# A hybrid encoder on one core: order of the down products, norm and gate loads at the layer boundary, scratch in two pools

## The chip, the cores and the metric

The kernel runs on one core of a Trainium2 chip. The metric is the device time of one execution in microseconds (us). A core has five engines that work side by side: PE (TensorE, matmuls; PEld is its loading of weights), DVE (VectorE), ACT (ScalarE), POOL (GpSimd) and SP (SyncE, which here only issues DMAs). Each runs its own list of instructions in order and waits on semaphores for the others.

## The reference

Two layers on x, 256 tokens of 2048 features, in fp32:

```
x = x + attention(rmsnorm(x));  x = x + swiglu(rmsnorm(x))     # layer 0
x = x + recurrent(rmsnorm(x));  x = x + swiglu(rmsnorm(x))     # layer 1
rmsnorm(x) = x * rsqrt(mean(x*x) + 1e-6) * g
swiglu(h)  = (silu(h @ w_gate) * (h @ w_up)) @ w_down          # 2048 -> 5632 -> 2048
recurrent(h): xb, gb = split(h @ w_in); xb = conv of width 4 (xb)
              a, i = gates of xb (blocks of 256 features, sigmoid)
              scans forward and backward, summed, times gelu(gb), then @ w_out
```

## The kernel before

**Precision and tiles.** Each fp32 operand is split into a high part (fp32r, a cast) and a low part (the rest); a product is three matmuls, high x high, high x low, low x high. Features lie in tiles of 128: 16 tiles for 2048. The 5632 hidden features of the FFN come in three parts of 12, 16 and 16 tiles (`PARTS`). A part is made of units of four tiles, each unit a pair of columns of 512 (one of w_gate, one of w_up), and is then multiplied by its rows of w_down, whose four columns of 512 are added to x (`x_tok`, tokens in partitions).

**Weights.** They stream in halves of 512 KB: SP issues the load (L114, tile raw, five buffers), ACT casts the high part (L123, hi), DVE subtracts the low part (L124, lo). PE uses a half for 12 matmuls of 128x512.

**project_pair** (matmul L294) multiplies a pair of columns at once: steps over k, one half per column and step, into two banks of sums (acc) per column. At the steps of `SEVEN` (2 and 5) it uses one level of Strassen: seven products instead of eight, from sums of the weights (wx on DVE, wxh a cast on ACT L271, wxl on DVE L272) and sums of the operands (hf); `merge` (L333 on) adds the results up into fg and fu. `pair_plan` gives the order: both columns in turn up to the last step of `SEVEN`, then one column's remaining two steps after the other's. **project_tokens** (matmul L247) multiplies one column by itself, one half after the other. `down` uses pairs for the 16-tile parts; the 12-tile part goes through `output`, which calls project_tokens column by column.

**Units.** At its end a unit turns its result by blocks (`turned`: DVE transposes into tb, L462, then 16 copies into tf, L468 on DVE and L470 on ACT) and splits it into four tiles (act; L795 on ACT, L796 on DVE), which the down product reads.

**Norm.** The norm before the recurrent layer (`nr`) works column by column while the last down ends: `add` squares (L426) and turns column c of x and writes four operands (xg; L418 on ACT, L419 on DVE). After the last column, `finish` takes the root (Ln and Exp on ACT, L541, three small operations on DVE, L484 to L486); `spread` scales the identity by it (ndg, L444) and puts a matmul with ones (L450) into PE's order after `NORM` tile steps; its result nrb (copied at L452) scales the projections afterwards.

**Recurrent layer.** Block 0's two feature tiles are projected first (`project_two`, matmuls L341 to L343, three of 128x256 per tile step): k tiles 0 to 7 for both, 8 to 11 for both, then 12 to 15, which are the operands of the last norm column. `conv_branch` does the convolution (L827 to L832) and splits the result (xs, L378 and L379). `load_gates` loads a gate's weights on SP (graw, L855), casts them on ACT (ghi, L856) and subtracts on POOL (glo, L857); four are loaded ahead. Gate products (three matmuls per tile, into pm) enter PE's order after `WHEN` tile steps of the projections that follow.

**Order and memory.** PE's order is the order of the program; `later(n, fn)` puts work into it n tile steps further on. The other engines are put in order by a scheduler that models the program. `follow` gives it an order without a semaphore. The FFN's scratch is one pool (`fp`: tb, tf, wx, fg, fu, forms), closed at the end of layer 0's FFN; the recurrent layer's pool (`rp`) is opened in the same place, so its first buffers wait for what lay there. The functions that the diff touches follow.

Of the kernel before, what the change touches and what calls it, by code (L numbers as in the profile page):

```python
# [18 lines left out]
P = 128  # L19
# [12 lines left out]
LAST_STEPS = (0, 1, 3, 2, 4, 5, 6, 7)  # L32
# [4 lines left out]
COMMON = {"nsq", "nr", "nrt", "rsq_s", "nj", "ndg", "nrb"}  # L37
EPS = 1e-6
# [5 lines left out]
NORM = 26  # L44
# [7 lines left out]
WHEN = (18, 25, 32, 39, 42, 46, 50, 54, 58, 60, 62, 64, 66, 70, 74)  # L52
WHEN_LAST = (5, 9, 13, 17, 19, 20, 21, 24, 24, 25, 26, 27, 33, 39, 39)
# [20 lines left out]
def trunk(ctx, tc, w, out):  # L74
# [60 lines left out]
    def pair_plan(steps, apart):  # L135
        m = 1 + steps.index(SEVEN[-1]) if apart else len(steps)
        return [(n, (0, 1)) for n in steps[:m]] + [(n, (j,)) for j in range(2) for n in steps[m:]]

    def unit_steps(first):
        return FIRST_STEPS if first else USUAL_STEPS, True  # L140

    def down_steps(p, second):
        last = p == len(PARTS) - 1
        return LAST_STEPS if second and last else USUAL_STEPS, True

    def ffn_order(l):
        units = [wide(f"w_gate{l}"), wide(f"w_up{l}")]
        seq, i = [], 0
        for p, n in enumerate(PARTS):
            for _ in range(n // FOUR):  # L150
                for k, cols in pair_plan(*unit_steps(i == 0)):
# [3 lines left out]
            if n != KT:  # L155
                seq += down
                continue
            for c in range(0, len(down), n):
                for k, cols in pair_plan(*down_steps(p, c > 0)):
                    seq += [down[c + n // 2 * j + k] for j in cols]  # L160
        return seq
# [95 lines left out]
    def seven_forms():  # L257
        load_half(*order[taken[0]])
        r1, w1 = flat(newest["raw"]), [flat(t) for t in newest["tiles"]]
        x, xh, xl = (fp[0].tile([P, 3, WIDE], t, tag=n, name=nm(n), bufs=1) for n, t in (("wx", F32), ("wxh", F32R), ("wxl", F32R)))  # L260

        def sums(raw):
            r2 = flat(raw)
            dve.tensor_tensor(x[:, 0, :], r2[:, 0, :], r1[:, 0, :], ALU.add)  # L264
            dve.tensor_tensor(r2[:, 0, :], r2[:, 0, :], r2[:, 1, :], ALU.add)
            dve.tensor_tensor(x[:, 1, :], r2[:, 0, :], r1[:, 0, :], ALU.add)
            dve.tensor_tensor(x[:, 2, :], x[:, 1, :], r1[:, 1, :], ALU.add)  # L267

# [3 lines left out]
        dve.tensor_tensor(xl, x, xh[:].bitcast(F32), ALU.subtract)  # L272
        taken[0] += 2
        return [[t[:, k, :] for t in w] for w, k in ((w1, 0), (w1, 1), (w2, 0), (w2, 1), ((xh, xl), 0), ((xh, xl), 1), ((xh, xl), 2))]

    def x_forms(h0, h1, tag):
        y = fp[0].tile([P, 8, P], F32, tag="tb", name=nm("tb"))
        for i, h in enumerate((h0, h1)):
            o, hi, lo = y[:, 2 * i : 2 * i + 2, :].rearrange("p a t -> p (a t)"), h[:, :S].bitcast(F32), h[:, S:].bitcast(F32)
            dve.tensor_tensor(o, hi, lo, ALU.add)  # L280
        for o, a, b in ((4, 1, 3), (5, 0, 4), (6, 0, 1), (7, 2, 5)):
            dve.tensor_tensor(y[:, o, :], y[:, a, :], y[:, b, :], ALU.subtract)
        t = fp[0].tile([P, 2, 4, P], F32R, tag=tag, name=nm(tag), bufs=1)
# [4 lines left out]
    def project_pair(xs, forms, order, middle, done):  # L288
        banks = [[new_acc() for _ in range(2)] for _ in range(2)]
        begun = set()  # L290

# [10 lines left out]
        steps = pair_plan(*order)  # L302
        seven = [n for n in order[0] if n in forms]
        for n, cols in steps:
            if n in forms:
# [6 lines left out]
                product(banks[0][0], tokens(2 * n + 1, 0), b21)  # L312
                product(banks[1][0], s4, b22)
# [3 lines left out]
                product(banks[0][1], tokens(2 * n + 1, 1), t4)  # L317
                if last:
                    middle(p1, q5, q6, q7)
            else:  # L320
                for j in cols:
                    half()
                    hi, lo = (flat(t) for t in newest["tiles"])
                    end = n == order[0][-1]
                    for a in range(2):
                        for k in range(2):
                            product(banks[j][a], tokens(2 * n + k, a), (hi[:, k, :], lo[:, k, :]), end and k == 1)
                    if end:
                        done(j, banks[j])

    def merge(p1, q5, q6, q7):
        g, u = (fp[0].tile([P, 2, WIDE], F32, tag=t, name=nm(t), bufs=1) for t in ("fg", "fu"))
# [72 lines left out]
    class Norm:  # L405
# [28 lines left out]
        def finish(self):  # L434
# [3 lines left out]
            self.rt = rsqrt(ms, "nr")  # L438


        def spread(self):
            dg = tmp("ndg", bufs=1)
            for a in range(2):
                dve.tensor_scalar(dg[:, a * P : (a + 1) * P], ident, self.rt[:, a : a + 1], None, ALU.mult)  # L444
# [8 lines left out]

            later(NORM, stage)

    def turned(src, both=True):
# [4 lines left out]
        for q in range(4):  # L463
            for i in range(4):
                o, y = f[32 * i : 32 * i + 32, q::4, :, :], b[32 * q : 32 * q + 32, :, i, :]
                y = y.rearrange("p a (k t) -> p a k t", k=FOUR)
                if i % 2 and both:
                    dve.tensor_copy(o, y)  # L468
                else:
                    act.copy(o, y)  # L470
# [4 lines left out]
    def open_ffn():  # L475
        fp[:] = [ffn_scope.enter_context(tc.tile_pool(name=nm("fp"), bufs=1))]
# [13 lines left out]
    def output(xs, norm=None, end=False, ready=0, close=None):  # L490
# [12 lines left out]
        if norm is not None:  # L503
            norm.finish()


    def down(xs, forms, p, norm=None, end=False):
        for c in (0, 2):
# [19 lines left out]
            project_pair(xs, forms, down_steps(p, c > 0), middle, done)  # L528
        if norm is not None:
            norm.finish()  # L530
# [244 lines left out]
    def ffn(norm, nxt):  # L775
        def unit(hid, forms, first):
# [12 lines left out]
            project_pair(norm.xs, norm.forms, unit_steps(first), lambda *banks: got.extend(merge(*banks)), done)  # L789
# [8 lines left out]
            for i, n in enumerate(SEVEN):  # L798
                if forms is not None and first <= 2 * n < len(hid):
                    forms[n] = x_forms(hid[2 * n], hid[2 * n + 1], f"hf{i}")  # L800

        for p, n in enumerate(PARTS):
            hid, forms = [], {} if n == KT else None
            for i in range(n // FOUR):
                unit(hid, forms, p == i == 0)
# [3 lines left out]
            if n == KT:  # L809
                down(hid, forms, p, nxt if last else None, last and nxt is None)  # L810
            else:
                output(hid)
# [4 lines left out]
    nr.spread()  # L817
# [3 lines left out]
    scope.append(rt.enter_context(tc.tile_pool(name="rp", bufs=2)))  # L821
# [99 lines left out]
    for b in range(-1, NBLK):  # L921
        blk, nxt = nxt, Block(b + 1) if b + 1 < NBLK else None
        if blk:
# [4 lines left out]
            when = WHEN if nxt else WHEN_LAST  # L928
# [11 lines left out]
    def end_recurrence():  # L940
        rt.close()
        scope.pop()
# [91 lines left out]
```

## Time and profile before

| | |
|---|---|
| median of 3 runs | 2022.96 us (2022.78 to 2024.07) |
| the profiled execution's own time | 2022.37 us |
| its span in the trace | 2020.6 us |
| PE busy | 1995.2 us (99%), 9944 matmuls |
| DVE, ACT, POOL busy | 1666.0, 1320.7, 165.7 us |
| mean granted PE clock | 0.993 |
| moved by DMA | 386.06 MB, 191 GB/s on the mean |

Times inside the trace count from the start of the span; the execution's own time is 1.8 us more than the span. In rows of groups and of the timeline, `out<-in` are the program's names, `x8` is a count, and what stands in brackets is the idle time before and the engine and line that ended it. In rows of waits stand the total, the number and the longest. The granted clock is PE's, as a share of full speed. Matmuls overlap, so the distance of their starts, and not their durations, is what one costs.

### The profile page before, as it was taken

What the parts mean: (1) busy time and instruction counts of PE and PEld (TensorE: products, weight loads), DVE (VectorE), ACT (ScalarE), POOL (GpSimd) and SP (SyncE); (2) the same over time, 40 slices, a digit from 0 to 9 for tenths busy, and PEclk for the clock granted to TensorE, in tenths of its full rate; (3) what the DMA queues carried; (4) which work ended last, traced back from release to release, by engine and by line L of the source; (5) the groups of instructions that cost most, each with busy time, mean ns of one, the idle gap of its engine ahead of it and who ended that gap; (6) DMA issues with size and microseconds to landing.
All of it is one profiled execution on the core that took longest, in us unless ns stands there. A gap on an engine that the chain in (4) does not pass through costs nothing.

```text
span 2020.6 us, 27860 instructions
## 1 busy us (share of the span) xinstructions
PE 1995.2 (99%) x9944; PEld 1696.2 (84%) x9944; DVE 1666.0 (82%) x2347; ACT 1320.7 (65%) x2054; POOL 165.7 (8%) x213
## 2 busy tenths in 40 slices
PE   9999999999999999999899999999999999999999
PEld 8898888878888888887799998888788888888887
DVE  8998788856888888889868887898657898878897
ACT  7666666644667546677688898667545766457663
POOL 1463000000000000000133330000000000000000
PEclk9999999999999999999999999999999999999999
DMA  8444665656555665555555555655566566665564
GB/s 320 158 137 140 193 200 187 207 168 198 192 195 187 219 208 188 190 195 192 188 163 188 178 179 174 200 188 187 195 185 202 185 204 206 203 192 187 196 222 146
DMA packets 109004, 386.06 MB, mean 191 GB/s; under 512 B 12225, under 2 KB 12993, under 8 KB 108737
## 3 DMA queue, kind: packets, MB, share of 16 engines
q1 hardware_dynamic: 108720, 384.26, 58.0%
q8 instruction: 78, 1.28, 0.3%
q14 instruction: 62, 0.50, 0.1%
q10 hardware_dynamic: 144, 0.02, 0.0%
HBM read 382.13 MB, written 2.10 MB: 190 GB/s over the span
## 4 chain that ended last, share of the span: by engine, by line
PE 52%; issue 41%; DVE 4%; DMA 1%; ACT 1%; POOL 0%; DVEq 0%; SPq 0%; ACTq 0%; POOLq 0%
PE acc L294 24%; PE acc L247 7%; PE acc L225 6%; PE pm L294 4%; PE acc L341 3%; PE acc L342 3%; PE acc L343 3%; DVE lo L124 2%; PE pm L342 1%; PE pm L343 1%; PE pm L341 1%; DMA raw<-in_w_up_dram 1%; ACT hi L123 0%; DMA graw<-in_w_gates_dram 0%; ACT tf L470 0%
## 5 line engine op out<-in xcount | busy, mean ns | idle before, releaser
L123 ACT CAST hi<-raw 128x1024 fp32r<-128x1024 f32 (+1 forms) x708 | 730.4, 1045 | 486.1 <-PE acc L294 314.1
L124 DVE TENSOR_TENSOR lo<-raw,hi 128x1024 fp32r<-128x1024 f32 (+1 forms) x708 | 857.4, 1228 | 172.0 <-ACT hi L123 169.9
L294 PE MATMUL acc<-hi,xg 128*128 128x512 f32 x2200 | 694.4, 389 | 2.3 <-DVE fg L783 1.2
L294 PEld LDWEIGHTS acc<-hi,xg 128*128 128x128 f32 x2200 | 412.9, 188 | 91.0 <-DVE fg L783 2.0
L294 PE MATMUL acc<-lo,xg 128*128 128x512 f32 x1100 | 427.9, 389 | 0.0
L247 PE MATMUL acc<-hi,act 128*128 128x512 f32 x896 | 283.4, 395 | 6.2 <-ACT act L795 5.4
L294 PE MATMUL acc<-hi,act 128*128 128x512 f32 x800 | 252.7, 389 | 0.0
L294 PEld LDWEIGHTS acc<-lo,xg 128*128 128x128 f32 x1100 | 206.5, 188 | 42.4
L247 PEld LDWEIGHTS acc<-hi,act 128*128 128x128 f32 x896 | 170.7, 191 | 43.8 <-ACT act L795 6.3
L470 ACT COPY tf<-tb 32x256 f32<-32x256 f32 x448 | 180.8, 403 | 12.7 <-DVE tb L462 6.1
L294 PEld LDWEIGHTS acc<-hi,act 128*128 128x128 f32 x800 | 150.2, 188 | 32.3 <-issue 0.7
L247 PE MATMUL acc<-lo,act 128*128 128x512 f32 x448 | 176.8, 395 | 0.0
L294 PE MATMUL acc<-lo,act 128*128 128x512 f32 x400 | 155.6, 389 | 0.0
L342 PE MATMUL acc<-xg,hi 128*128 128x256 f32 x512 | 146.7, 286 | 2.0 <-DVE xg L419 1.9
L341 PE MATMUL acc<-xg,hi 128*128 128x256 f32 x512 | 146.8, 287 | 1.0 <-ACT xg L418 1.0
L343 PE MATMUL acc<-xg,lo 128*128 128x256 f32 x512 | 146.2, 285 | 0.0
L264 DVE TENSOR_TENSOR wx<-raw,raw 128x512 f32<-128x512 f32 x60 | 41.5, 692 | 123.7 <-DMA raw<-in_w_up_dram 97.1
L225 PE MATMUL acc<-xg,hi 128*128 128x512 f32 x384 | 127.1, 400 | 0.5 <-ACT hi L123 0.5
L271 ACT CAST wxh<-wx 128x1536 fp32r<-128x1536 f32 x60 | 88.9, 1482 | 49.6 <-DVE wx L267 46.7
L272 DVE TENSOR_TENSOR wxl<-wx,wxh 128x1536 fp32r<-128x1536 f32 x60 | 104.8, 1747 | 10.5 <-ACT wxh L271 10.5
L342 PEld LDWEIGHTS acc<-xg,hi 128*128 128x128 f32 x512 | 99.7, 195 | 2.5 <-DVE xg L419 2.4
L341 PEld LDWEIGHTS acc<-xg,hi 128*128 128x128 f32 x512 | 99.8, 195 | 1.5 <-ACT xg L418 1.3
(239 smaller groups left out, 2728.4 us busy)
## 6 DMA issues: line engine op xcount, KB each, us to landing
raw<-in_w_gate_dram SPq DMA_DIRECT2D x176, 512.0 KB, 4.0
raw<-in_w_up_dram SPq DMA_DIRECT2D x176, 512.0 KB, 4.4
raw<-in_w_down_dram SPq DMA_DIRECT2D x176, 512.0 KB, 4.2
raw<-in_w_in_dram SPq DMA_DIRECT2D x64, 512.0 KB, 4.6
raw<-in_w_qv_dram SPq DMA_DIRECT2D x40, 512.0 KB, 4.3
raw<-in_w_o_dram SPq DMA_DIRECT2D x32, 512.0 KB, 3.6
raw<-in_w_out_dram SPq DMA_DIRECT2D x32, 512.0 KB, 4.3
graw<-in_w_gates_dram SPq DMA_DIRECT2D x32, 256.0 KB, 3.6
```

Source lines behind the costliest of these rows:

```text
L123: newest["cast"] = act.copy(hi[:, sl, :], raw[:, sl, :])
L124: dve.tensor_tensor(lo[:, sl, :], raw[:, sl, :], hi[:, sl, :].bitcast(F32), ALU.subtract)
L225: pe.matmul(o, w, x, start=(k == 0 and not part), stop=(k == total - 1 and not part))
L247: pe.matmul(accs[a], x, wt[:, k, :], start=(k0 + k == 0 and n == 0), stop=(end and k == 1 and n == 2))
L264: dve.tensor_tensor(x[:, 0, :], r2[:, 0, :], r1[:, 0, :], ALU.add)
L271: act.copy(xh, x)
L272: dve.tensor_tensor(xl, x, xh[:].bitcast(F32), ALU.subtract)
L294: pe.matmul(acc, a, b, start=id(acc) not in begun, stop=last and i == 2)
L341: pe.matmul(o, hi, x[:, :S], start=start, stop=False)
L342: pe.matmul(o, hi, x[:, S:], start=False, stop=False)
L343: pe.matmul(o, lo, x[:, :S], start=False, stop=stop)
L470: act.copy(o, y)
```

## The change

1. The 12-tile down of either layer goes through `down`, so in pairs, without seven forms: four steps for both columns, then the last two column by column (`SHORT`, `down_plan`). Banks of sums are taken when first used.
2. Layer 0's last down takes its second pair of columns without seven forms and one column after the other (`alone`). `LAST_STEPS`, an order of steps for the last downs' second pairs, is gone.
3. The root (`finish`) is taken in `add` of the last column, ahead of its block copies; for `nr` the diagonal (`spread`) too, and the copies on ACT follow the Exp, those on DVE the diagonal. `NORM` is 20 instead of 26.
4. The FFN's scratch is two pools, `fq` (tb, tf) and `fp` (the rest), and the recurrent layer's too, `rq` (cb, xc, gl) and `rp` (the rest).
5. Block 0's four gates enter PE's order after 24, 30, 36 and 42 tile steps instead of 18, 25, 32 and 39.

```diff
-LAST_STEPS = (0, 1, 3, 2, 4, 5, 6, 7)
+SHORT = 6
+LOW = {"cb", "xc", "gl"}
-NORM = 26
+NORM = 20
+WHEN_FIRST = (24, 30, 36, 42) + WHEN[4:]
...
-        pl = tp if tag in COMMON else scope[-1]
+        pl = tp if tag in COMMON else scope[-2] if tag in LOW else scope[-1]
...
+    def pair_plan(steps, together):
+        return [(n, (0, 1)) for n in steps[:together]] + [(n, (j,)) for j in range(2) for n in steps[together:]]
...
+    def down_plan(n, alone):
+        if alone:
+            return pair_plan(range(n), 0)
+        return pair_plan(range(n), SHORT - 2 if n == SHORT else 1 + SEVEN[-1])
...
-        x, xh, xl = (fp[0].tile([P, 3, WIDE], t, tag=n, name=nm(n), bufs=1) for n, t in (("wx", F32), ("wxh", F32R), ("wxl", F32R)))
+        x, xh, xl = (fp[1].tile([P, 3, WIDE], t, tag=n, name=nm(n), bufs=1) for n, t in (("wx", F32), ("wxh", F32R), ("wxl", F32R)))
...
-        banks = [[new_acc() for _ in range(2)] for _ in range(2)]
+        banks = [[], []]
+        def bank(j, a):
+            while len(banks[j]) <= a:
+                banks[j].append(new_acc())
+            return banks[j][a]
...
         def add(self, c):
             for a in range(2):
                 act.activation(tmp("nj", (P, WIDE), bufs=1), x_tok[:, a, c, :], AF.Square, accum_out=self.sums[:, a, c : c + 1])
-            for f in turned(x_tok[:, :, c, :]):
+            behind = self.finish() if c == NCOL - 1 else None
+            for f in turned(x_tok[:, :, c, :], True, behind):
...
             self.rt = rsqrt(ms, "nr")
+            if not self.seven:
+                return prev[0], self.spread()
...
+                turn = dve.tensor_copy if i % 2 and both else act.copy
+                n = turn(o, y)
+                if behind is not None:
+                    follow(n, behind[i % 2])
...
-        fp[:] = [ffn_scope.enter_context(tc.tile_pool(name=nm("fp"), bufs=1))]
+        fp[:] = [ffn_scope.enter_context(tc.tile_pool(name=nm(s), bufs=1)) for s in ("fq", "fp")]
...
-            project_pair(xs, forms, down_steps(p, c > 0), middle, done)
-        if norm is not None:
-            norm.finish()
+            alone = norm is not None and c > 0
+            project_pair(xs, {} if alone else forms, down_plan(len(xs) // 2, alone), middle, done)
...
-            if n == KT:
-                down(hid, forms, p, nxt if last else None, last and nxt is None)
-            else:
-                output(hid)
+            down(hid, forms, nxt if last else None, last and nxt is None)
...
     ffn_scope.close()
-    nr.spread()
...
-    scope.append(rt.enter_context(tc.tile_pool(name="rp", bufs=2)))
+    scope.extend([rt.enter_context(tc.tile_pool(name=s, bufs=2)) for s in ("rq", "rp")])
...
-            when = WHEN if nxt else WHEN_LAST
+            when = WHEN_FIRST if not blk.b else WHEN if nxt else WHEN_LAST
```

Three places show what this moves. The first is PE in layer 0's 12-tile down; the numbers tell buffers apart; hi and lo are the parts of a half of w_down, act_3986 (after: act_3989) is the last tile of the second unit, act_4332 (after: act_4335) the first of the third. Before:

```order
L247 MATMUL acc_4345<-hi_4401,act_3986 128x512
L247 MATMUL acc_4345<-lo_4402,act_3986 128x512
L247 MATMUL acc_4345<-hi_4401,act_3986 128x512
L247 MATMUL acc_4344<-hi_4419,act_4332 128x512
L247 MATMUL acc_4344<-lo_4420,act_4332 128x512
```

and after:

```order
L299 MATMUL acc_4380<-hi_4478,act_3989 128x512
L299 MATMUL acc_4380<-lo_4479,act_3989 128x512
L299 MATMUL acc_4380<-hi_4478,act_3989 128x512
L299 MATMUL acc_4353<-hi_4496,act_4335 128x512
L299 MATMUL acc_4353<-lo_4497,act_4335 128x512
```

Before, the third unit's first tile is read after four halves of one column, 48 matmuls into the down; after, it is read after four halves of either column, 96 matmuls into it.

The second is ACT where layer 0's last down ends; nj are the squares, tf the block copies of column 3, xg its operands, the rows that write rsq_s and nr the Ln and the Exp. Before:

```order
L426 ACTIVATE nj_9075,nsq_3278<-x_tok 128x512
L123 CAST hi_9392<-raw_9391 128x1024
L470 COPY tf_9078<-tb_9077 32x2x128 x8
L418 ACTIVATE xg_9097<-tf_9078,pk 128x256
L418 ACTIVATE xg_9100<-tf_9078,pk 128x256
L418 ACTIVATE xg_9103<-tf_9078,pk 128x256
L418 ACTIVATE xg_9106<-tf_9078,pk 128x256
L541 ACTIVATE rsq_s_9113<-nrt_9109 128x2
L541 ACTIVATE nr_9112<-rsq_s_9113 128x2
L856 CAST ghi_9294<-graw_9295 128x512
L452 COPY nrb_9249<-pm_9246 128x256
```

and after:

```order
L430 ACTIVATE nj_9051,nsq_3281<-x_tok 128x512
L125 CAST hi_9329<-raw_9328 128x1024
L546 ACTIVATE rsq_s_9057<-nrt_9053 128x2
L546 ACTIVATE nr_9056<-rsq_s_9057 128x2
L476 COPY tf_9067<-tb_9066 32x2x128 x8
L125 CAST hi_9372<-raw_9371 128x1024
L459 COPY nrb_9211<-pm_9208 128x256
L422 ACTIVATE xg_9086<-tf_9067,pk 128x256
L422 ACTIVATE xg_9089<-tf_9067,pk 128x256
L422 ACTIVATE xg_9092<-tf_9067,pk 128x256
L422 ACTIVATE xg_9095<-tf_9067,pk 128x256
```

Ln and Exp have moved ahead of the copies, the norm's copy nrb ahead of the operands, and no gate cast stands here.

The third is SP's queue of loads: raw are halves of weights, graw the gates' weights. Before:

```order
L114 DMA raw_9634<-in_w_in_dram 128x1024
L114 DMA raw_9672<-in_w_in_dram 128x1024
L855 DMA graw_9295<-in_w_gates_dram 128x512
L855 DMA graw_9301<-in_w_gates_dram 128x512
L855 DMA graw_9307<-in_w_gates_dram 128x512
L855 DMA graw_9313<-in_w_gates_dram 128x512
L114 DMA raw_9722<-in_w_in_dram 128x1024
L855 DMA graw_9418<-in_w_gates_dram 128x512
```

and after:

```order
L116 DMA raw_8809<-in_w_down_2_dram 128x1024
L856 DMA graw_9275<-in_w_gates_dram 128x512
L856 DMA graw_9281<-in_w_gates_dram 128x512
L116 DMA raw_8827<-in_w_down_2_dram 128x1024
L116 DMA raw_8845<-in_w_down_2_dram 128x1024
L856 DMA graw_9287<-in_w_gates_dram 128x512
L116 DMA raw_8901<-in_w_down_2_dram 128x1024
L856 DMA graw_9293<-in_w_gates_dram 128x512
L116 DMA raw_8921<-in_w_down_2_dram 128x1024
L856 DMA graw_9416<-in_w_gates_dram 128x512
```

Before, the gate loads stand behind the first twelve loads of w_in; after, six of them stand among the second half of the loads of layer 0's last w_down; the sixth follows one load behind the last row.

More of the change, by code (lines that the diff above doesn't have):

```diff
@@ L300, in tokens @@
             return [xs[k][:, o + a * P : o + (a + 1) * P] for o in (0, S)]
-        steps = pair_plan(*order)
-        seven = [n for n in order[0] if n in forms]
-        for n, cols in steps:
+        seven = [n for n, cols in plan if n in forms]
+        for n, cols in plan:
             if n in forms:
@@ L775, in ffn, with unit @@
     def ffn(norm, nxt):
-        def unit(hid, forms, first):
+        def unit(hid, forms, parts, first):
             got = []
@@ L941, in end_recurrence @@
         rt.close()
-        scope.pop()
+        del scope[-2:]
         ln_exp_tables()
```

71 lines of the change are left out of this document (29 added, 42 removed).

## The prediction

> **What bounds the kernel now.** I read the busy times first, then what TensorE (PE) waited for, then busy times by stretch, and last single places in order of time.
>
> ```profile
> span 2020.6 us, 27860 instructions
> PE 1995.2 (99%) x9944; PEld 1696.2 (84%) x9944; DVE 1666.0 (82%) x2347; ACT 1320.7 (65%) x2054; POOL 165.7 (8%) x213
> ...
> 418.00:950.00 532.00, 531.71 (x2344) 439.45 (x2343) 441.25 (x538) 329.16 (x447) 0.00 (x0) 1.00 0.60 196
> 1014.50:1200.00 185.50, 185.50 (x1556) 185.50 (x1555) 152.45 (x249) 165.23 (x281) 69.39 (x87) 1.00 0.57 179
> ```
>
> PE is the bound, and over long stretches it has no gap. A stretch's row gives its length, then busy time and instructions of PE, PEld, DVE, ACT and POOL, then the granted clock. The first stretch holds 128x512 matmuls: one takes 532.00 / 2344 = 0.227 us. The second holds 128x256 ones: 185.50 / 1556 = 0.119 us. So the time falls only with fewer matmuls or with less lost between them. Where is it lost?
>
> ```profile
> PE acc L247 <- ACT act L795: 5.4, 2, 2.7
> PE pm L294 <- DVE wxl L272: 2.2, 1, 2.2
> PE acc L342 <- DVE xg L419: 1.9, 1, 1.9
> PE pm L341 <- DVE xs L378: 1.8, 1, 1.8
> PE pm L341 <- ACT hi L123: 1.7, 1, 1.7
> PE acc L294 <- DVE fg L783: 1.2, 2, 0.6
> PE acc L294 <- DVE fu L786: 1.2, 4, 0.4
> PE pm L450 <- DVE ndg L444: 1.1, 1, 1.1
> ...
> 406.00:418.00 12.00, 8.76 (x25) 6.18 (x24) 6.27 (x9) 6.15 (x11) 0.00 (x0) 0.72 0.38 133
> 950.00:956.00 6.00, 3.81 (x18) 2.81 (x17) 5.96 (x9) 1.84 (x2) 0.00 (x0) 1.00 0.70 238
> 982.00:997.00 15.00, 10.88 (x59) 9.86 (x58) 10.61 (x28) 9.80 (x25) 0.50 (x5) 0.77 0.44 142
> 1003.60:1014.50 10.90, 7.03 (x34) 6.16 (x34) 9.67 (x16) 5.77 (x9) 3.11 (x6) 0.69 0.62 198
> 1447.00:1459.00 12.00, 9.04 (x26) 6.38 (x25) 5.88 (x8) 6.52 (x12) 0.00 (x0) 0.72 0.40 132
> ```
>
> A wait's row gives total, times and longest. The large ones lie in the five stretches below them, and in four of these the clock sinks to about 0.7: such a wait costs more than itself. By the pitches, 406 to 418 needs 25 x 0.227 = 5.7 us of its 12.0: 6.3 are lost; 1447 to 1459 needs 5.9, so 6.1. There the down product of the first FFN part (12 tiles) starts, in either layer. 982 to 997 needs 55 x 0.119, and about 0.06 for each of four short matmuls of the norm, together 6.8: 8.2 lost. 1003.6 to 1014.5 needs 34 x 0.119 = 4.05: 6.85 lost. These two are the start of the recurrent layer and its first gates.
>
> **Part A: the 12-tile down in pairs.**
>
> ```profile
> 400.33 6.63 ACT L470 COPY tf<-tb 32x256 f32<-32x256 f32 x16 [0.72 <-DVE tb L462]
> 406.99 1.99 ACT L123 CAST hi<-raw 128x1024 fp32r<-128x1024 f32 x2
> 408.89 1.32 ACT L795 CAST act<-tf 128x256 fp32r<-128x256 f32 x4
> ...
> 410.34 1.43 DVE L796 TENSOR_TENSOR act<-tf,act 128x256 fp32r<-128x256 f32 x4
> ...
> 406.25 0.39 PE L247 MATMUL acc<-hi,act 128*128 128x512 f32 x1
> 409.34 0.51 PE L247 MATMUL acc<-hi,act 128*128 128x512 f32 x1 [2.71 <-ACT act L795]
> ```
>
> From 406.25 PE stands before tile 8, which the last unit hands over only after 16 block copies and two casts of halves; its last low part ends at 410.34 + 1.43 = 411.8. Before the change 48 matmuls of the down stand ahead of tile 8, after it 96. So the down starts at about 406.5 - 48 x 0.227 = 395.6, and tile 8 is needed at 395.6 + 96 x 0.227 = 417.4, 5.6 us after its last part is there. What hides the wait is 48 more matmuls on tiles that are ready; a half of the weights still serves 12 matmuls (2.72 us), so the loads keep their pace, and ACT and DVE keep their order up to these casts. I count the loss as gone: -6.3 and -6.1, **-12.4**. Bounds: nothing saved if PE waits elsewhere; 0.4 more at each place, since matmuls cut by a stretch's edges are counted whole.
>
> What it adds: a pair holds four banks of sums where a column held two. The rows of L783 and L786 are such waits at the starts of pairs: 2.4 us in all over some 30 pairs, 0.08 a pair. With six more starts (four pairs in the 12-tile downs, two single columns at the end of layer 0) I take **+0.4**; bounds 0 and 6 x 0.6 = 3.6.
>
> **Part B: layer 0's last pair without seven forms, a column at a time.**
>
> ```profile
> 952.21 1.75 DVE L272 TENSOR_TENSOR wxl<-wx,wxh 128x1536 fp32r<-128x1536 f32 x1
> ...
> 951.43 0.39 PE L294 MATMUL pm<-wxh,hf 128*128 128x512 f32 x1
> 954.01 0.50 PE L294 MATMUL pm<-wxl,hf 128*128 128x512 f32 x1 [2.19 <-DVE wxl L272]
> ```
>
> One matmul goes from 951.43 to 954.01: 2.58 - 0.23 = 2.35 lost. No sums, no wait: -2.35. Each form spares one product in eight, three matmuls, so two forms less add 6 x 0.227 = +1.36. Together **-1.0**. What is late next is a low part of a half, which DVE writes beside the norm of column 1; with DVE rid of 1.75 us of wxl and four additions for each form I put that at nothing, and bound it by the old wait, +2.35.
>
> **Part C: the boundary.** T is the end of the last down.
>
> ```profile
> 986.34 3.30 ACT L470 COPY tf<-tb 32x256 f32<-32x256 f32 x8 [0.77 <-DVE xg L419]
> 990.02 1.71 ACT L418 ACTIVATE xg<-tf,pk 128x256 fp32r<-128x256 f32 x4 [0.38 <-DVE tf L468]
> 991.63 0.19 ACT L541 ACTIVATE rsq_s<-nrt 128x2 f32<-128x2 f32 x1
> ...
> 980.58 0.69 DVE L522 TENSOR_TENSOR x_tok<-x_tok,acc 128x512 f32<-128x512 f32 x1
> 987.54 2.38 DVE L468 COPY tf<-tb 32x256 f32<-32x256 f32 x8
> ...
> 977.04 0.28 PE L341 MATMUL acc<-xg,hi 128*128 128x256 f32 x1
> ```
>
> Before, T is 977.04. Columns 2 and 3 end only two halves (5.4 us) apart, so column 2's copies and operands still hold both engines after T: column 3 is added to x only at 980.58 + 0.69 (T+4.2), its ACT copies start at T+9.3, its operands at T+13, and the root behind them at T+14.6. After, column 2 ends eight halves (8 x 2.72 = 21.8 us) ahead of T and is out of the way. My chain from T: both additions by T+1.0, squares, casts and transposes to T+3.8, Ln and Exp (two of 0.2) to T+4.5, ACT's eight copies (3.3) to T+7.8, a cast (1.05) and the norm's copy (0.4) to T+9.2, four operands (1.7) to T+10.9; on DVE root, diagonal and copies (2.4) to T+8.8, a low half (1.2), the four low parts (1.7) to T+11.7. PE multiplies operands 0 to 11 first, 72 matmuls of 0.119 and the norm's four: it asks for operand 12 at T+9 and for its low part at once, each of the four coming some 0.4 us late. I take 1.5 us of waits for 8.2: **-6.7**. Bounds: 0 left, or half of 8.2.
>
> The norm's matmuls, moved 6 tiles earlier, come at T+7.2 and want the diagonal of T+6.4: no wait in place of the 1.1 us.
>
> ```profile
> 992.64 6.96 SPq L855 DMA_DIRECT2D graw<-in_w_gates_dram  x4
> ...
> 996.70 2.55 POOL L857 TENSOR_TENSOR glo<-graw,ghi 128x512 fp32r<-128x512 f32 x2 [4.05 <-ACT ghi L856]
> 1003.78 1.54 POOL L857 TENSOR_TENSOR glo<-graw,ghi 128x512 fp32r<-128x512 f32 x1 [0.59 <-ACT ghi L856]
> ...
> 1004.12 1.36 DVE L378 CAST xs<-xc 128x256 fp32r<-128x256 f32 x1
> 1008.24 0.29 DVE L378 CAST xs<-xc 128x256 fp32r<-128x256 f32 x1
> ```
>
> At the first gates PE waited for a half (1.7) and for xs (1.8). The four gate loads were issued from 992.64 only, since their buffers lay on tb and tf; so four casts (0.62 each) and four subtractions on POOL stood among the convolution's work, and beside POOL one cast on DVE took 1.36 for 0.29. After, the loads go out during the last down, and that work is done before T. The gates come six tiles (6 x 3 x 0.119 = 2.1 us) later as well. The chain from T puts the second xs at T+23.3 and the first gate at T+22.1 to 22.5: about 0.8 us left of 6.85, **-6.0**. Bounds: 0, or the waits' 3.5 - 2.1 = 1.4 with the slow clock, some 3.
>
> The four POOL subtractions now stand beside DVE's last column. The row of 1.36 shows 1.07 us lost at one of them. The Trainium skill, "SBUF — State Buffer", section "Who interferes with whom", says that a GpSimd operation that reads SBUF shuts out a DVE operation with two SBUF inputs for its whole length. The row agrees with a block to the end of the subtraction (1003.78 + 1.54 = 1005.3). It speaks against the change, since DVE has the low halves to write there.
>
> **The sum.** -12.4 + 0.4 - 1.0 - 6.7 - 6.0 = -25.7 on the profiled execution's own 2022.37: 1996.7. The median shown, 2022.96, is 0.6 above it: **1997.2**. Restoring the natural order of steps in layer 1's last pair costs nothing: the same order runs without loss in the pairs of 418 to 950.
>
> **The rivals.**
> 1. *The boundary keeps half* (0.22): the copies now follow the root, so operand 12 is late by the whole of the root's delay, and the clock sinks again. For it: a wait of 1.9 came before a stretch of 0.77. Against: the 2.19 at 951 left the clock at 1.00, and mine come in pieces. Half of 8.2 + 6.85 is 7.5, where I count 2.3: +5.2, 2002.4. The Trainium skill, "TensorE: Matmul & The Clock Gate", Part 1, has half rate only after an idle window of about 3.4 us; by it these waits would cost only themselves. The rows speak against it: 2.71 was enough at 409.
> 2. *POOL shuts out DVE* (0.08) in the last column, four times 1.3 = 5.2 us; ACT's column 2 work with its casts is some 23.7 us by these rows, which leaves a low half some 2.4 us of the ring's cover, so PE waits 2.8: 2000.0.
> 3. *The pairs only move the wait* (0.07), as 4 tiles of the last unit still come late or the banks are held: +12.4, 2009.6. Against: 5.6 us to spare.
> 4. *The gate loads stop the stream* (0.05): on SP's queue the six now stand among the last down's halves, and each waits for a buffer that POOL or DVE frees.
>
> ```profile
> SPq L855 <- POOL glo L857: 33.0, 28, 3.5
> ```
>
>    Such a wait is 1.2 on the mean, 3.5 at most. Five raw buffers hold 5 x 2.72 = 13.6 us of PE's work. To end slower than before, the six must hold the queue 13.6 + 25.7 = 39.3 us, 6.6 each; at 7.5 each the loss is 45 - 13.6 = 31.4, and the time 2028.6. Against: twice the longest seen.
> 5. *It does nothing here* (0.01): 2023. The order of the matmuls excludes it nearly.
>
> **How the numbers follow.** My forecast has 0.57, 1993 to 2000.5: the bounds of what is left (0 to 2.3 at the boundary) and of the banks. Rivals 1 and 2 lie up to 2005, with the slow clock once more; so 1993 to 2005 holds about 0.85, and I leave out rivals 3, 4 and 5. A measurement tells 0.2%, 4 us, from no change. Faster by more: 0.57 + 0.22 + 0.08 + 0.07 = 0.94, less 0.01 for rivals worse than priced: 0.93; within: 0.02; slower: 0.05.
>
> **What would show it.** A: no wait of PE for act and clock 1.00 through 395 to 420 and at the second layer's down; wrong if a wait for act, hi or lo of over 1 us stands there. B: no wxl behind column 1; six matmuls more. C: root ahead of copies, waits for xg below 2 us together, clock 1.00 behind T; gate loads and subtractions before T, casts on DVE at 0.29, and the wait at the first gate under 1 us. Wrong as a whole if SP's queue shows waits of the gate loads above 5 us with PE waiting for hi or lo in the last down.

## The result, and the profile after

The changed kernel takes 1995.07 us (median of 4 runs, 1994.69 to 1996.29); the kernel before takes 2022.87 us (median of 4 runs, 2021.08 to 2024.07). The ratio is 0.9864, 95% interval 0.9847 to 0.9881: 27.8 us, 1.4% faster. The forecast was 1997.2 in a range of 1993 to 2005.

The lines of the page and the waits of TensorE (PE) in the changed kernel. Its source lines stand some five further down: L299 is the matmul of pairs (before L294), L345 to L347 those of the recurrent layer (L341 to L343), L788 and L791 the bank readers of a unit (L783 and L786), L528 those of a down.

```profile
span 1993.1 us, 27849 instructions
PE 1981.8 (99%) x9950; PEld 1686.4 (85%) x9950; DVE 1652.8 (83%) x2329; ACT 1317.0 (66%) x2051; POOL 168.6 (8%) x213
...
PE acc L299 <- DVE fg L788: 1.0, 2, 0.5
PE pm L401 <- POOL ones L398: 1.0, 1, 1.0
PE acc L225 <- ACT hi L125: 0.9, 1, 0.9
PE acc L299 <- DVE x_tok L528: 0.9, 1, 0.9
PE acc L299 <- DVE fu L791: 0.7, 3, 0.3
PE pm L346 <- DVE pT L725: 0.7, 1, 0.7
PE acc L346 <- DVE xg L423: 0.6, 1, 0.6
```

The waits for act, wxl, xs, hi at the gates and ndg have gone from the list; the six matmuls more are there (9950 for 9944). What is left at the places of the change is one wait for xg. New is one of 0.9 us for x_tok, a bank not yet read; it stands at 1695.82, in a 16-tile down of layer 1. The same five stretches, found by their work (start of the 12-tile downs, end of layer 0's last down, boundary, first gates):

```profile
395.00:420.00 25.00, 25.00 (x112) 20.71 (x111) 15.53 (x19) 17.03 (x30) 0.00 (x0) 1.00 0.57 187
900.00:968.90 68.90, 68.90 (x306) 57.05 (x305) 63.25 (x92) 51.55 (x86) 6.97 (x4) 1.00 0.68 225
968.90:985.00 16.10, 15.35 (x124) 14.87 (x123) 14.22 (x32) 12.86 (x26) 0.20 (x4) 1.00 0.44 152
985.00:996.00 11.00, 11.00 (x93) 10.84 (x92) 10.18 (x19) 6.57 (x9) 1.63 (x7) 1.00 0.65 207
1417.00:1445.00 28.00, 28.00 (x125) 23.20 (x124) 17.31 (x21) 17.92 (x30) 0.00 (x0) 1.00 0.60 200
```

PE is without a gap in four of the five, and the granted clock is 1.00 in all of them.

To see where the 27.5 us of the two profiled executions (2022.37 and 1994.88) went, I took six marks from PE's starts: the first matmul of layer 0's FFN; T, the first 128x256 matmul behind its last down; the 96th and the 250th 128x256 matmul from T on (the boundary, then the first gates); the first matmul of layer 1's FFN and the last matmul.

| from mark to mark, us | before | after | difference |
|---|---|---|---|
| layer 0's FFN, to T | 708.88 | 701.68 | -7.20 |
| T to the 96th | 20.14 | 13.22 | -6.92 |
| the 96th to the 250th | 25.50 | 18.60 | -6.90 |
| the 250th to layer 1's FFN | 286.86 | 286.62 | -0.24 |
| layer 1's FFN, to the last matmul | 706.87 | 701.06 | -5.81 |

Up to layer 0's FFN the difference is -0.6; nothing is changed there. These marks serve for the experiments too. A stretch in which the program is the same varies by up to 3 us from execution to execution (layer 1's FFN took 701.06 in the changed kernel, 699.91 in e3 and 702.81 in e5, which do not touch it), and the waits for fu and x_tok vary with it. So an edit of 1 us is read at its own place, not in the median.

The chain behind T in the changed kernel, in order of time (start, duration, engine):

```profile
973.15 0.20 ACT L546 ACTIVATE rsq_s<-nrt 128x2 f32<-128x2 f32 x1
973.38 0.20 ACT L546 ACTIVATE nr<-rsq_s 128x2 f32<-128x2 f32 x1
973.49 3.30 ACT L476 COPY tf<-tb 32x256 f32<-32x256 f32 x8
...
978.02 1.71 ACT L422 ACTIVATE xg<-tf,pk 128x256 fp32r<-128x256 f32 x4
...
975.00 0.48 DVE L451 TENSOR_SCALAR ndg<-ident,nr 128x128 f32<-128x128 f32 x2
975.51 2.39 DVE L476 COPY tf<-tb 32x256 f32<-32x256 f32 x8
...
979.61 0.38 PE L346 MATMUL acc<-xg,hi 128*128 128x256 f32 x1 [0.64 <-DVE xg L423]
```

T is 969.24 here. Ln and Exp come 3.9 us behind T (before: 14.6), the copies start at T+4.2 (before: T+9.3), and the diagonal is done at T+6.2, ahead of PE's request.

### The profile page after: what moved, and what is told of

Read it like the earlier page. It is cut to its first block, busy times and chain, and to the rows that moved or that the text cites. A ratio compares the mean times of both kernels' runs of the same rounds, so it can differ in the third digit from the quotient of the medians.

```text
span 1993.1 us, 27849 instructions
## 1 busy us (share of the span) xinstructions
PE 1981.8 (99%) x9950; PEld 1686.4 (85%) x9950; DVE 1652.8 (83%) x2329; ACT 1317.0 (66%) x2051; POOL 168.6 (8%) x213
## 4 chain that ended last, share of the span: by engine, by line
PE 84%; DVE 8%; DMA 3%; issue 2%; ACT 1%; SPq 0%; POOL 0%; DVEq 0%; ACTq 0%
PE acc L299 51%; PE acc L247 8%; PE pm L299 6%; PE acc L225 5%; DVE lo L126 4%; PE acc L346 3%; PE acc L345 3%; PE acc L347 3%; DMA raw<-in_w_up_dram 2%; PE pm L347 1%; PE pm L346 1%; PE pm L345 1%; DMA raw<-in_w_down_dram 1%; ACT hi L125 1%; DVE fg L788 0%
## 5 line engine op out<-in xcount | busy, mean ns | idle before, releaser
L299 PE MATMUL acc<-hi,xg 128*128 128x512 f32 x2200 | 695.2, 390 | 1.8 <-DVE fg L788 1.0
L299 PEld LDWEIGHTS acc<-hi,xg 128*128 128x128 f32 x2200 | 412.9, 188 | 91.5 <-ACT wxh L271 2.9
L299 PE MATMUL acc<-lo,xg 128*128 128x512 f32 x1100 | 428.0, 389 | 0.0
L299 PE MATMUL acc<-hi,act 128*128 128x512 f32 x1212 | 379.3, 389 | 0.9 <-DVE x_tok L528 0.9
L299 PEld LDWEIGHTS acc<-hi,act 128*128 128x128 f32 x1212 | 227.5, 188 | 49.3 <-issue 1.8
L299 PEld LDWEIGHTS acc<-lo,xg 128*128 128x128 f32 x1100 | 206.5, 188 | 42.5
L299 PE MATMUL acc<-lo,act 128*128 128x512 f32 x606 | 235.8, 389 | 0.0
L476 ACT COPY tf<-tb 32x256 f32<-32x256 f32 x448 | 180.7, 403 | 10.9 <-DVE tb L470 4.7
L345 PE MATMUL acc<-xg,hi 128*128 128x256 f32 x512 | 144.9, 283 | 0.1
L347 PE MATMUL acc<-xg,lo 128*128 128x256 f32 x512 | 144.4, 282 | 0.0
L299 PEld LDWEIGHTS acc<-lo,act 128*128 128x128 f32 x606 | 113.8, 188 | 23.4
L858 POOL TENSOR_TENSOR glo<-graw,ghi 128x512 fp32r<-128x512 f32 x32 | 51.4, 1605 | 777.5 <-DMA graw<-in_w_gates_dram 740.1
```

The costliest lines, as they stand in the source:

```text
L299: pe.matmul(acc, a, b, start=id(acc) not in begun, stop=last and i == 2)
L345: pe.matmul(o, hi, x[:, :S], start=start, stop=False)
L347: pe.matmul(o, lo, x[:, :S], start=False, stop=stop)
L476: n = turn(o, y)
L858: pool.tensor_tensor(lo, raw, hi[:].bitcast(F32), ALU.subtract)
```

## The experiments

All edits start from the changed kernel (1995.07). Times are medians, with the ratio to the kernel before; local figures go by the marks.

**e1: the 12-tile down in columns again.**

```diff
+            if n != KT:
+                seq += down
+                continue
...
-            down(hid, forms, nxt if last else None, last and nxt is None)
+            if n == KT:
+                down(hid, forms, nxt if last else None, last and nxt is None)
+            else:
+                output(hid)
```

> The changed kernel with the 12-tile down of both layers back in single columns; all else stays. Theory (the wait is hidden by 48 more matmuls on ready tiles): both waits for act return at 2.7 us each, the clock sinks behind them to about 0.72, some 6.5 us lost at each place: +13 us, about 2008. Rival (the gain has another source, such as fewer starts or the loads' pace): the waits return at most in part, below +5 us, under 2000.

2007.82 us, 0.9923 (0.9910 to 0.9937): +12.75. PE at the third unit's first tile, and the stretch around it:

```profile
408.66 0.50 PE L250 MATMUL acc<-hi,act 128*128 128x512 f32 x1 [2.71 <-ACT act L803]
...
395.00:420.00 25.00, 21.64 (x82) 16.94 (x81) 13.80 (x19) 14.84 (x27) 0.00 (x0) 0.86 0.49 156
```

The wait returns to the hundredth (2.71), the clock sinks to 0.86 over the 25 us, and 82 matmuls fit where 112 did. Both FFNs are longer (by 6.0 and 7.7), the boundary is as in the changed kernel (13.18 and 18.59). This part is worth 13 of the 27.8 us.

**e7 and e8: how much cover is needed.** One or two steps for both columns instead of four, so 60 or 72 matmuls ahead of the third unit instead of 96.

```diff
-        return pair_plan(range(n), SHORT - 2 if n == SHORT else 1 + SEVEN[-1])
+        return pair_plan(range(n), SHORT - 5 if n == SHORT else 1 + SEVEN[-1])
```

(e8 has `SHORT - 4`.)

> The changed kernel with the 12-tile down taking one step for both columns and five for each alone, so that 60 matmuls instead of 96 stand ahead of the third unit's first tile. Theory (cover in matmuls against the time of the casts, and a clock that sinks only behind a wait of some 1.9 us or more): PE asks for tile 8 at 408.8, its high part is there at 408.9, its low part at 410.3; it waits about 1.1 us at each of the two places and the clock stays 1.00: +2 us, about 1997. Rival (any wait there lets the clock sink): +3.4 us more at either place, 2001 to 2004. Rival (the pairs as such remove the wait): 0.

> The changed kernel with two steps of the 12-tile down for both columns, so 72 matmuls ahead of the third unit's first tile. Theory (cover in matmuls): PE asks at 395.15 + 72 x 0.227 = 411.5, the last low part of the first two tiles is there at about 410.7: no wait for act, the time of the changed kernel within 0.3 us. Rival (the margin must be larger, as casts of halves slip in between): a wait of 0.5 us or more for act, lo or hi at either place.

e7: 1997.58, 0.9875 (0.9861 to 0.9888), +2.5. e8: 1995.54, 0.9859 (0.9844 to 0.9874), no difference, and no wait for act in its list. In e7, the casts and low parts of the tiles and PE's wait:

```profile
408.20 1.32 ACT L800 CAST act<-tf 128x256 fp32r<-128x256 f32 x4
...
409.66 1.43 DVE L801 TENSOR_TENSOR act<-tf,act 128x256 fp32r<-128x256 f32 x4
...
408.99 0.40 PE L299 MATMUL acc<-lo,act 128*128 128x512 f32 x1
410.13 0.73 PE L299 MATMUL acc<-hi,act 128*128 128x512 f32 x2 [0.75 <-DVE act L801]
```

PE has the high part at once and stands 410.13 - 408.99 - 0.23 = 0.9 us for the low part, in layer 1 as well, with the clock at 1.00. So what counts is the number of matmuls ahead against the time of the casts: 48 leave 2.7 us, 60 leave 1, 72 none. The pairs as such remove nothing, and the 96 of the change hold 24 in reserve.

**e2 and e10: what column 2 must be clear of.** e2 gives layer 0's last pair its seven forms back, and with them both columns in turn; e10 leaves the forms out but takes both columns in turn up to step 5.

```diff
-            alone = norm is not None and c > 0
+            alone = False
```

(with `down_plan(n // 2, False)` in the order of the loads), and in e10:

```diff
-            return pair_plan(range(n), 0)
+            return pair_plan(range(n), 1 + SEVEN[-1])
```

> The changed kernel with layer 0's last pair again with seven forms and both columns in turn up to step 5. Theory (column 2 out of the way is what frees the boundary): 6 matmuls fewer (-1.4), the wait for wxl behind column 1 back (+2.35), and column 2's copies and operands stand in front of column 3's, so PE waits 4 to 6 us for xg and the clock may sink behind it: +5 to +8 us in all, 2000 to 2003. Rival (the root ahead of the copies and the later gates free the boundary): only -1.4 + 2.35 = +1 us, about 1996.

> The changed kernel with layer 0's last pair without seven forms still, but both columns in turn up to step 5 (column 2 ends 5.4 us ahead of column 3 instead of 21.8). Theory (column 2's copies and operands in front of column 3's are what delays the boundary): waits of PE for xg of 4 us and more and a sunken clock behind T, +5 to +8 us, 2000 to 2003. Rival (the seven forms delayed it, by DVE's time and by the scratch that kept the gate loads back): waits for xg below 2 us, within 1.5 us of the changed kernel.

e2: 2007.82, 0.9922 (0.9910 to 0.9935), +12.75. e10: 2001.45, 0.9895 (0.9881 to 0.9909), +6.4. By the marks T to the 96th took 22.55 in e2 and 17.99 in e10 (13.22 in the changed kernel): +9.3 and +4.8. First ACT and PE of e2, then ACT and PE of e10:

```profile
972.24 0.62 ACT L857 CAST ghi<-graw 128x512 fp32r<-128x512 f32 x1 [2.52 <-DMA graw<-in_w_gates_dram]
...
982.88 0.58 PE L345 MATMUL acc<-xg,hi 128*128 128x256 f32 x1 [5.84 <-ACT xg L422]
```

```profile
966.92 3.30 ACT L476 COPY tf<-tb 32x256 f32<-32x256 f32 x8
...
971.20 1.71 ACT L422 ACTIVATE xg<-tf,pk 128x256 fp32r<-128x256 f32 x4
...
978.91 0.20 ACT L546 ACTIVATE rsq_s<-nrt 128x2 f32<-128x2 f32 x1 [1.94 <-DVE nrt L442]
...
980.32 1.01 PE L457 MATMUL pm<-ndg,ones 128*128 128x128 f32 x3 [3.14 <-DVE ndg L451]
```

In e10 T is 969.83, and column 2's copies and operands fill ACT from 966.9 to 972.9: the root comes at T+9, and PE stands 3.1 us, not for xg, as I had written, but for the diagonal, which it asks for first. The place and the size were as the theory had them. e2 goes beyond both expectations, since it undoes two things: the sums of the seven forms keep the scratch that the gate buffers now lie on, so the gate loads are late again (968.48 and later, where the changed kernel has 920.03 to 936.90) and ACT stands 2.52 us at a cast of gate weights, until T+1.1, in front of the squares and the copies. Column order alone is 4.8 us at this place, the forms with the late loads 4.5 more. The rest of e10's +6.4 lies in the pair itself: it takes 45.17 us for 43.52, with one wait of 1.31 us for a bank (x_tok) at 930.21.

**e3 and e6: the root and the norm's place.** e3 has the root behind the fourth column's operands and `NORM` 26, e6 only `NORM` 26.

```diff
-NORM = 20
+NORM = 26
...
-            behind = self.finish() if c == NCOL - 1 else None
-            for f in turned(x_tok[:, :, c, :], True, behind):
+            for f in turned(x_tok[:, :, c, :]):
...
+            if c == NCOL - 1:
+                self.finish()
```

> The changed kernel with the root behind the fourth column's operands again and its matmuls after 26 tile steps. Theory (column 2 was the load, the root is a small matter): operand 12 comes about 1 us sooner and its wait goes, the diagonal comes 1.5 to 2.5 us after PE asks for it: +1 to +2 us, clock stays 1.00 or nearly. Rival (the root's place is what frees the boundary): waits for ndg of 3 us and more with the clock near 0.77 as before the change, +5 us, about 2000.

> The changed kernel with the norm's matmuls after 26 tile steps instead of 20 (the root stays ahead of the copies). Theory (the norm's matmuls had no wait to lose; their copy on ACT stands ahead of operand 12): without it operand 12 is ready 0.36 us sooner, the wait for xg falls from 0.75 to about 0.4 us, no wait for ndg: -0.4 us, not to be told from no change. Rival (their place matters): a new wait of 1 us or more in the convolution for nrb, seen as a wait of PE for xs at the first gate with the clock below 1.00.

e3: 1995.75, 0.9866 (0.9851 to 0.9881); e6: 1995.35, 0.9861 (0.9846 to 0.9875). Neither median can be told from the changed kernel's. Locally e3 loses: T to the 96th takes 15.76 (+2.5), and one wait stands there:

```profile
980.99 0.71 PE L458 MATMUL pm<-ndg,ones 128*128 128x128 f32 x4 [2.21 <-DVE ndg L452]
...
966.00:985.00 19.00, 16.79 (x115) 16.00 (x114) 14.15 (x31) 12.37 (x25) 0.20 (x4) 0.91 0.51 169
```

That is the size of the theory (1.5 to 2.5 late), not of the rival, but the clock did sink once, to 0.91. In e6 the theory fell: T to the 96th is 13.55, 0.3 longer, and the waits for xg are 0.50 and 0.67, more than in the changed kernel. PE reaches operand 12 sooner when the norm's matmuls do not stand ahead of it, and so waits longer for it; the operand itself is there no sooner (PE goes on at T+9.3 in both), so the copy on ACT is not what counts.

**e4, e5 and e12: gate weights and gates.** e4 puts each layer's scratch back into one pool, e5 the gates back to the earlier steps, e12 both.

```diff
-        fp[:] = [ffn_scope.enter_context(tc.tile_pool(name=nm(s), bufs=1)) for s in ("fq", "fp")]
+        fp[:] = [ffn_scope.enter_context(tc.tile_pool(name=nm("fp"), bufs=1))] * 2
...
-    scope.extend([rt.enter_context(tc.tile_pool(name=s, bufs=2)) for s in ("rq", "rp")])
+    scope.extend([rt.enter_context(tc.tile_pool(name="rp", bufs=2))] * 2)
```

```diff
-WHEN_FIRST = (24, 30, 36, 42) + WHEN[4:]
+WHEN_FIRST = WHEN
```

> The changed kernel with each layer's scratch in one pool again, so that the gate weights' buffers lie on the FFN's scratch; gates stay 6 tiles later. Theory (early loads and later gates share the work): gate loads go out only behind T, four casts and four POOL subtractions stand among the convolution, one or two DVE casts take 1.3 us instead of 0.3, PE waits 1 to 2 us at the first gates and the clock may sink: +1.5 to +4 us, 1996.5 to 1999. Rival (the later gates suffice): no wait of PE there, within 0.5 us of the changed kernel.

> The changed kernel with block 0's gates back at 18, 25, 32 and 39 tile steps; gate weights are still loaded early. Theory (the second xs sets the first gate): PE asks 2.1 us sooner, waits 1.7 to 2.1 us in two or three pieces for xs, which gives back what the delay cost; the clock stays 1.00 or sinks for one stretch of 3.4 us: 0 to +2 us on the whole, 1995 to 1997. Rival (the delay is worth the half of what the gates gained): +3.4 us and more, over 1998.5.

> The changed kernel with one pool of scratch and block 0's gates back at 18, 25, 32 and 39: both of what belongs to the gates undone. Theory (early loads are the larger part, and the delay of the gates saves its 2.1 us of waits whether or not the loads are early): one pool alone cost 7.1, early gates alone 3.0; together 9 to 11 us, 2004 to 2006. Rival (both undo the same wait): no more than 7.5 us, 2002.5 or less.

| 96th to 250th, us | gates later | gates early |
|---|---|---|
| two pools | 18.60 (changed kernel) | 22.26 (e5) |
| one pool | 25.07 (e4) | 25.41 (e12) |

The medians: e4 2002.14, 0.9897 (0.9883 to 0.9910), +7.1; e5 1998.12, 0.9877 (0.9863 to 0.9892), +3.0; e12 2000.11, 0.9882 (0.9865 to 0.9898), +5.0. e4 is above both of its expectations; e5's median lies between its two. Its ACT, DVE and PE at the gates:

```profile
985.68 1.28 ACT L857 CAST ghi<-graw 128x512 fp32r<-128x512 f32 x2 [2.48 <-DMA graw<-in_w_gates_dram]
986.86 0.56 ACT L830 ACTIVATE acc<-cb,pk 128x256 f32<-128x256 f32 x1
...
987.46 0.49 DVE L833 SCALAR_TENSOR_TENSOR acc<-cb,pk,acc 128x256 f32<-128x256 f32 x1 [2.19 <-ACT acc L830]
992.73 1.35 DVE L382 CAST xs<-xc 128x256 fp32r<-128x256 f32 x1
...
994.14 0.58 PE L345 MATMUL pm<-xs,ghi 128*128 128x256 f32 x1 [1.91 <-DVE xs L382]
995.54 0.58 PE L346 MATMUL pm<-xs,ghi 128*128 128x256 f32 x1 [0.82 <-DVE xs L383]
```

ACT stands 2.48 us at a gate cast whose load is not there; the convolution's operation (L830) is next in its order, DVE stands 2.19 us for that, and the second xs is late by it. What I had counted were the casts' own durations and DVE's work beside POOL, and that is there (1.35 for 0.29 at the second xs); what I had not counted is an engine that waits in order at a load, 2.19 us on DVE. How the 6.5 us divide between the two was not tried. In e12 it is late nearly as much (PE goes on at T+25.8, in e4 at T+26.8), and PE merely arrives sooner and waits longer. (That e12's median is below e4's is not of this place: in the profiled executions layer 1's FFN took 700.2 in e12 and 703.4 in e4, which no edit tells apart there.) So the delay of the gates is worth 3.7 us at its place when the loads are early and 0.3 when they are late: both belong to one wait, and the rival of e12 was right. In e5 the waits are 0.41, 0.84 and 0.34 us, but the clock sinks:

```profile
989.95 0.38 PE L345 MATMUL pm<-xs,ghi 128*128 128x256 f32 x1 [0.84 <-DVE xs L382]
990.67 0.38 PE L346 MATMUL pm<-xs,ghi 128*128 128x256 f32 x1 [0.34 <-DVE xs L383]
...
985.00:1010.00 25.00, 23.42 (x179) 22.81 (x178) 13.04 (x25) 16.82 (x29) 8.77 (x16) 0.93 0.48 154
```

The sinking is about half of the 3.7 us: 0.07 of 25 us, some 1.75 us, beside 1.6 us of waits.

**e9 and e11: a seven form in the 12-tile downs.** At step 2, for both pairs of columns (e9) or the second alone (e11).

```diff
-                if parts == KT and first <= 2 * n < len(hid):
+                if (parts == KT or i == 0) and first <= 2 * n < len(hid):
```

In e11 also:

```diff
-            project_pair(xs, {} if alone else forms, down_plan(len(xs) // 2, alone), middle, done)
+            project_pair(xs, {} if alone or (len(xs) < KT and not c) else forms, down_plan(len(xs) // 2, alone), middle, done)
```

> The changed kernel with a seven form at step 2 of the 12-tile downs too. Theory (PE's count sets the time as long as DVE keeps up): 4 forms, each 3 matmuls of 0.227 us fewer: -2.7 us, 1992.3. Rival (DVE, with 4 sums, a low part of the sums, 4 operations of the merge and 4 additions more in each pair, falls behind with the low parts of the halves): waits of PE for lo or wxl of 2 us and more in the 12-tile downs, 1995 or slower.

> The changed kernel with a seven form at step 2 of the second pair of columns of the 12-tile downs alone. Theory (in the first pair DVE's extra work stood ahead of the low parts of the last unit's tiles; in the second pair nothing is due): two forms, 6 matmuls fewer, no wait for act: -1.4 us, 1993.7. Rival (DVE has no room there either): waits of PE for wxl, lo or x_tok of 1 us or more behind the second pair's start, 1995 or slower.

e9: 1995.82, 0.9865 (0.9850 to 0.9881). e11: 1994.88, 0.9857 (0.9842 to 0.9872). DVE and PE of e9 at the third unit's first tiles:

```profile
416.09 0.68 DVE L339 TENSOR_TENSOR fu<-pm,fg 128x512 f32<-128x512 f32 x1
416.69 1.22 DVE L126 TENSOR_TENSOR lo<-raw,hi 128x1024 fp32r<-128x1024 f32 x1
417.83 1.43 DVE L801 TENSOR_TENSOR act<-tf,act 128x256 fp32r<-128x256 f32 x4
...
418.30 0.73 PE L299 MATMUL acc<-hi,act 128*128 128x512 f32 x2 [1.77 <-DVE act L801]
```

The merge's operations stand ahead of the low parts of the tiles on DVE, and PE waits 1.77 and, in layer 1, 1.15 us: 2.9 of waits for 2.7 of matmuls saved. The rival had the time and DVE as the cause; it named lo and wxl, and the wait is for act. In e11 no such wait stands; the FFNs are 0.03 and 0.55 us shorter, where the count says 0.68 each. That is not more than the scatter of those stretches, so whether e11 beats the changed kernel stays open; no version tried is clearly faster than it.

## Why the prediction was right

**Part A** was right by its own steps: the loss goes whole, the 48 matmuls more are what hides it (e1, e7, e8), and ACT's and DVE's order kept. By the starts of PE the two losses were 6.65 and 6.54 us (18 matmuls from 406.25 to 416.99, 21 from 1447.63 to 1458.94) instead of 6.3 and 6.1, which is why 12.4 was 0.8 short. The +0.4 for banks did not come: at the six new starts PE has no wait in the trace. The waits for fg, fu and x_tok are 2.6 us in all, 2.4 before, and lie at other places (311.75, 801.62, 1331.88, 1695.82 and 1822.96). Rival 3 (the pairs only move the wait) did not come true: PE has no wait in either 12-tile down.

**Part B**: -1.0 was forecast. By PE's starts layer 0's last pair of columns takes 44.65 us before (186 matmuls) and 43.52 after (192): -1.13, without a wait. The experiments that leave the pair so all have 43.52. Layer 0's FFN as a whole is shorter by 7.20, where -6.65 and -1.13 make -7.8; the difference is within the scatter of that stretch.

**Part C, T to the first gates**: the chain from T held within some 0.4 us at each step named (ACT's copies to T+7.8, here 976.79 - 969.24 = 7.55; the diagonal T+6.4, here 6.24; ACT's operands T+10.9, here 10.5; the four low parts T+11.7, here 11.5). 1.5 us of waits were expected; PE loses 1.2, read from its starts at 978.20, 978.59 and 979.61. The term was -6.7, and T to the 96th is 6.92 shorter. That column 2 was the load, and the clear 21.8 us the remedy, is shown by e10 (+4.8); the place of the root is the smaller part (e3: +2.5 for root and norm together).

**Part C, the gates**: 0.8 us were expected to be left and 0.2 is (two starts that come 0.1 late, at 991.81 and 992.03): the second xs is whole at T+22.5, not T+23.3. The term was -6.0 and measures -6.90, the largest miss of the sum. The step that was wrong in kind is how I divided it. I let early loads and later gates each take a share; the runs show one wait for the second xs, which the late loads cause (in e4's trace by holding ACT in order, and by DVE's work beside POOL), and the delay of the gates bears only on what the loads leave (e5, e12).

Added up, the terms were too small by 0.8, 0.4, 0.1, 0.2 and 0.9 us, all to the same side, and the median came out 2.1 below the forecast; no two errors hid each other.

**POOL beside DVE**, rival 2: the four subtractions came some 45 to 33 us ahead of T. POOL of the changed kernel, and DVE next to it:

```profile
926.17 1.82 POOL L858 TENSOR_TENSOR glo<-graw,ghi 128x512 fp32r<-128x512 f32 x1 [0.73 <-ACT ghi L857]
931.59 2.25 POOL L858 TENSOR_TENSOR glo<-graw,ghi 128x512 fp32r<-128x512 f32 x1 [3.60 <-ACT ghi L857]
...
926.87 3.37 DVE L476 COPY tf<-tb 32x256 f32<-32x256 f32 x8
...
933.23 1.70 DVE L126 TENSOR_TENSOR lo<-raw,hi 128x1024 fp32r<-128x1024 f32 x1
934.85 2.70 DVE L423 SCALAR_TENSOR_TENSOR xg<-tf,pk,xg 128x256 fp32r<-128x256 f32 x4
```

DVE's eight copies take 3.37 for 2.39, its four operands 2.70 for 1.67, one low half 1.70 for 1.22, and POOL's subtractions up to 2.25 for 1.30: each side gives way in its turn, as the rule of the Trainium skill that I cited, "SBUF — State Buffer", section "Who interferes with whom", has it for operations that need the shared ports. The rule as I quoted it is for two SBUF inputs, and the cast of 1.36 from which I priced it has one; the low half here (raw and hi) is a case with two. DVE lost some 2.5 us, half of the price that I gave, and PE waited for none of it. The mechanism was there; it was cheaper than I took it, and covered.

**Gate loads on SP's queue**, rival 4: in the changed kernel the longest wait of a gate load is 4.1 us, for the addition of fu to x_tok, below the 6.6 each from which it would have decided, and PE waited for no half in layer 0's last down. **Rival 1** (half of the boundary's loss stays) did not come true: the rests are 0.64 us and less, and the clock stays at 1.00. My reason against it, that the waits come in pieces, does not hold, though: pieces add up (e5, and the last section). What kept the clock is that they add up to 0.75 us here.

## What to carry to other kernels

Where the bounding engine waits for the last piece of a product, count how much work on pieces that are ready can be put ahead of it; the wait goes when that work outlasts the chain behind the piece, here between 60 and 72 matmuls, and more cover brings nothing. A load that an in-order engine waits for costs what stands behind it on that engine, and not only the duration of its cast: see to it that the buffer is free early, and look at what else lies on it. Two edits that shorten one wait don't add up: undo each by itself and both together before dividing a gain among them.

## What the runs showed of the hardware

A short wait can cost as much again by the clock, and its length alone does not say when. Among 128x512 matmuls, waits of 1.77 (e9) and 2.19 us (before) left the clock at 1.00 and one of 2.71 did not; among 128x256 matmuls, 2.21 in one piece (e3) and even 0.41, 0.84 and 0.34 within 3 us (e5) were enough for a stretch at half rate. The Trainium skill, "TensorE: Matmul & The Clock Gate", Part 1, has the half rate after an idle window of about 3.4 us; no wait in these runs is that long but one (5.84, e2).

The traces say more. Before the last matmul the clock sinks to 0.50 thirteen times in the 14 traces, for 3.41 or 6.83 us each, and within a trace the falls lie on a fixed grid of slots of 3.41 us: in the kernel before, the first and the last, at 409.69 and 1450.76, are 305 slots apart. Laid on that grid, the wait of 1.77 in e9 falls on two slots (the grid is taken from the fall behind its last matmul, at 1991.03), while the three waits of e5 fall into one:

```profile
414.07:417.48 3.41, 2.46 (x11) 1.69 (x9) 3.41 (x5) 3.41 (x7) 0.00 (x0) 1.00 0.57 171
417.48:420.89 3.41, 2.59 (x11) 2.17 (x12) 3.41 (x8) 0.60 (x1) 0.00 (x0) 1.00 0.75 225
...
987.89:991.30 3.41, 1.83 (x11) 1.22 (x10) 3.31 (x8) 0.91 (x2) 0.13 (x2) 1.00 0.65 202
991.30:994.71 3.41, 3.41 (x18) 3.41 (x18) 1.02 (x3) 2.58 (x4) 1.53 (x3) 0.50 0.36 126
```

PE is idle for 0.95 and 0.82 us in the two slots of e9, and for 1.58 in the first slot of e5. The 2.19 of the kernel before is parted too, into 0.59 and 1.60. Over all traces, each of the twelve slots at full clock with 1.65 us of idle time or more was followed by one at half; of those with less, only the 1.58 of e5 was, and 1.60 (before) and 1.52 (e2) were not. So in these runs what counts is the sum of PE's idle time within one slot, with a border near 1.6 of 3.41 us. The ends of matmuls are modelled, so the border is rough, and whether it is the same for both sizes of matmul was not tried. The grid lies differently to the program in each execution, so a wait of some 2 us can sink the clock in one and not in the next.
